# Loading the weight through GpSimd's queue instead of SyncE's, behind the first load of x

## The chip, the cores and the metric

The kernel runs on one core of a Trainium2 chip. The metric is the time of one execution on the device in microseconds, lower is better. Profiles come from one execution under the hardware profiler.

## What is computed

```python
batch, m, k, n = 16, 512, 1024, 768
def reference(x, weight, scale, add_value):
    return (scale * np.matmul(x, weight) + add_value).astype(np.float32)
```

All arrays are float32: x has 8192 rows of 1024 (33.6 MB), the weight is 1024 x 768 (3.1 MB), add_value and the output have 8192 rows of 768 (25.2 MB each). `scale` is 0.1.

## The kernel before

The 8192 rows are 64 tiles of 128 rows. x is laid out so that a partition holds 16 successive rows of a group of 2048; a load of 8 tiles (4,096 KB) therefore brings 32 KB to each partition in one run. The weight stays on the chip as eight slices of 128 x 768 in bf16 (`w_bf`). The buffers are `xs` (16 tiles of x), `ao` (32 tiles of add_value, over which the result is written in place, and whose last eight tiles first hold the float32 weight), `va` (two buffers of x in bf16, four tiles each, called a move), `xt` (four tiles of transposed x) and `mm` (four accumulators in PSUM).

Each engine has its own program, and they meet at semaphores only:

- SyncE (`sync_engine`) issues nearly all transfers, in the order of the list `STREAM`: `("w", 0, 4)` is half of the weight (slices 0 to 3), `("x", 8, 8)` eight tiles of x from tile 8 on, `"a"` is add_value, `"o"` is a store. The first load of x (tiles 0 to 7) is issued ahead of that list, at line 239. The weight is issued at line 111, x at 118, add_value at 130, stores at 143; waits ahead of them are in `need`, line 102. All of these go through one hardware queue, q1. A load of add_value waits until the one before it has landed, a load of x until the casts have freed its place.
- ScalarE and GpSimd (`mover`, cast at line 163) copy x to bf16 in eight instructions per move each, in an order that makes the later transpose work on blocks of 32 x 32. Each takes half of the partitions' blocks, and each waits for the load (`x_sem`) and for a free `va` (`turned`).
- VectorE (`vector_engine`) first casts the weight in two halves (`cast_w`, line 171), each behind the landing of its half (`w_sem`). Then it transposes the moves from `va` to `xt`, half a move per instruction (`turn`, line 178); the first half of a move waits for both movers. Between transposes it takes finished accumulators, two tiles at a time, and makes `scale * mm + ao` (`finish`, line 187).
- TensorE (`product`, line 210) waits for all eight slices of the cast weight, and then for each pair of tiles for the transposes and for free accumulators.
- GpSimd besides issues three stores of tiles 8 and 15 (`store_pair`, line 95) after its first 64 casts; they use the software queue q0. They are its only transfers.

The end of the list orders the last transfers: `("a", 56, 8), ("o", 32, 16), ("o", 48, 12), ("o", 60, 4)`. The store of tiles 48 to 59 (4,608 KB) waits for the results of tile 59, the last store (1,536 KB) for those of tile 63.

Of the kernel before, what the change touches and what calls it, by code (L numbers as in the profile page):

```python
# [16 lines left out]
VA_BUFS = 2  # L17
MOVE = 4
AHEAD = 4
HALF_BLOCK, PAST, SYNC_AT = 64, 4, 4  # L20

STREAM = [
# [13 lines left out]
def kernel(  # L36
# [8 lines left out]
    nc = tc.nc  # L45
# [15 lines left out]
    w_v = weight.rearrange("(c p r) n -> p c (r n)", p=P, r=2)  # L61

    def rows(view, s, n):
        assert s // R == (s + n - 1) // R
        return view[:, s // R, s % R:s % R + n, :]
# [5 lines left out]
    ao = const.tile([P, A_SLOTS, N], fp32, name="ao")  # L71
# [6 lines left out]
    w_sem = [tc.alloc_semaphore(f"w{i}") for i in range(2)]  # L78
    x_sem = [tc.alloc_semaphore(f"x{i}") for i in range(X_SLOTS // MOVE)]
# [8 lines left out]
    W_AT = A_SLOTS - KJ  # L88

    def slot(t):  # L90
        return t % A_SLOTS

    def store_pair(eng, p, n):
        assert PAIR.stop <= R and PAIR.stop <= A_SLOTS
        eng.dma_start(out_v[p:p + n, 0, PAIR, :], ao[p:p + n, PAIR, :]).then_inc(aside_sem, 16)  # L95

    def sync_engine(eng):
        groups, stores, known = 0, [], {}

        def need(sem, value):  # L100
            if known.get(sem, 0) < value:
                eng.wait_ge(sem, value)  # L102
                known[sem] = value

        for at, (op, s, n) in enumerate(STREAM):
            if at == SYNC_AT:
                eng.addr_align(HALF_BLOCK, offset=PAST, max_nops=0)
            last = s + n - 1
            if op == "w":
                dst = ao[:, W_AT + s:W_AT + s + n, :].rearrange("p (c r) n -> p c (r n)", r=2)  # L110
                move, sem = eng.dma_start(dst, w_v[:, s // 2:(s + n) // 2, :]), w_sem[s // 4]
            elif op == "x":
                k = s % X_SLOTS
                if last >= X_SLOTS:
                    moved = 8 * (last + 1 - X_SLOTS) // MOVE
                    need(by_act, moved)
                    need(by_pool, moved)
                move = eng.dma_start(xs[:, k:k + n, :], rows(x_v, s, n))  # L118
                sem = x_sem[k // MOVE]
            elif op == "a":  # L120
                if groups:
                    need(a_sem, 16 * groups)
                if last == A_SLOTS - 1:
                    need(casts, KJ)
                if s <= PAIR.start + A_SLOTS <= last:
                    need(aside_sem, 16 * len(BY_POOL))
                if s >= A_SLOTS:
                    i = next(j for j, (a, b) in enumerate(stores) if a <= last - 1 - A_SLOTS < a + b)
                    need(o_sem[i % 2], 16 * (i // 2 + 1))
                move = eng.dma_start(ao[:, slot(s):slot(s) + n, :], rows(add_v, s, n))  # L130
                sem = a_sem
                groups += 1
            elif op == "a+":
                need(a_sem, 16 * groups)
                eng.sem_inc(a_sem, 16 * (n // G - 1))
                groups += n // G - 1
                continue
            else:
                i = len(stores)
                if i > 1:  # L140
                    need(o_sem[i % 2], 16 * (i // 2))
                need(made, MADE + last + 1)
                move = eng.dma_start(rows(out_v, s, n), ao[:, slot(s):slot(s) + n, :])
                sem = o_sem[i % 2] if s < ENDING else end_sem
                stores.append((s, n))
            move.then_inc(sem, 16)
            if op == "x" and n == 2 * MOVE:
                eng.sem_inc(x_sem[k // MOVE + 1], 16)

    def mover(eng, copy, parity, count, go=None, first=0, turns=T // X_SLOTS):  # L150
        if go is None:
            eng.preload_act_table(mybir.ActivationFunctionType.Copy)  # L152
        with eng.Fori(16 * (first + 1), 16 * (first + turns) + 1, 16) as i:  # L153
            for q in range(X_SLOTS // MOVE):
                eng.wait_ge(x_sem[q], i)
                eng.wait_ge(turned, i + (4 * q - 12) if q < 3 else i)  # L156
                if go is not None:
                    eng.sem_inc(go, 1)  # L158
                k = MOVE * q
                src = xs[:, k:k + MOVE, :].rearrange("p i (c b k) -> p (i c) b k", b=4, k=64)  # L160
                for a in (parity, parity + 2):
                    for b in range(4):
                        copy(va[q % VA_BUFS][32 * b:32 * b + 32, :, a, :],  # L163
                             src[32 * a:32 * a + 32, :, b, :]).then_inc(count, 1)

    def vector_engine(eng):
        ao_g = ao.rearrange("p (g t) n -> p g t n", t=G)

        def cast_w(s, n):
            eng.wait_ge(w_sem[s // 4], 16)  # L170
            eng.tensor_copy(w_bf[:, s:s + n, :], ao[:, W_AT + s:W_AT + s + n, :]).then_inc(casts, n)  # L171

        def turn(move, half, moves=None):
            if half == 0:
                eng.wait_ge(by_act, moves)
                eng.wait_ge(by_pool, moves)  # L176
            q = 2 * half * KC
            eng.transpose(  # L178
                xt[:, 2 * half:2 * half + 2, :, :].rearrange("p i c m -> p (i c m)"),
                va[move % VA_BUFS][:, q:q + 2 * KC, :, :].bitcast(fp32).rearrange("p c a k -> p (c a k)"),  # L180
            ).then_inc(turned, 2)

        def finish(pair, at, products):
            eng.wait_ge(done, products)
            a = ao_g[:, at, 2 * pair:2 * pair + 2, :]
            q = 2 * (pair % 2)
            eng.scalar_tensor_tensor(  # L187
                a, mm[:, q:q + 2, 0:N], float(scale), a,
                op0=mybir.AluOpType.mult, op1=mybir.AluOpType.add).then_inc(made, 2)

        def group(i, at, last):
            eng.wait_ge(a_sem, i)
            for p in range(4):
                finish(p, at, i + (4 * p - 12) if p < 3 else i)
                if p < 2 or not last:
                    turn(1 if p < 2 else 0, p % 2, i + 8 if p == 2 else i)

        cast_w(0, 4)
        cast_w(4, 4)
        turn(0, 0, 8)  # L200
        turn(0, 1)
        with eng.Fori(16, 2 * T, 16) as i:
            group(i, bass.ds((i // 16 + A_SLOTS // G - 1) % (A_SLOTS // G), 1), False)
        s = slot(T - G) // G
        group(2 * T, slice(s, s + 1), True)
# [12 lines left out]
    def tensor_engine(eng):  # L218
        eng.sem_inc(x_sem[1], 16)
        eng.sem_inc(turned, TURNED)  # L220
        eng.sem_inc(made, MADE)
        eng.wait_ge(casts, KJ)
        with eng.Fori(TURNED + 2, TURNED + 2 + T, XT_TILES) as i:
            for q in range(XT_TILES):
                if q % 2 == 0:
                    eng.wait_ge(turned, i + q if q else i)
                    eng.wait_ge(made, i + q if q else i)
                for j in range(KJ):
                    x2 = xt[:, q, j // 2, :].bitcast(bf16).rearrange("p (m r) -> p r m", r=2)
                    m = product(eng, mm[:, q, :], x2[:, j % 2, :], w_bf[:, j, :], j)  # L230
                if q % 2:
                    m.then_inc(done, 4)
# [4 lines left out]
    s, n = FIRST  # L237
# [4 lines left out]
    with tc.tile_critical(no_gpsimd_drain=True):  # L242
        sync_engine(nc.sync)
        mover(nc.scalar, nc.scalar.copy, 0, by_act)
        mover(nc.gpsimd, nc.gpsimd.tensor_copy, 1, by_pool, pool_go, 0, TURN_AT)
        nc.gpsimd.wait_ge(made, MADE + PAIR.stop)
        for p, n in BY_POOL:
            store_pair(nc.gpsimd, p, n)
        nc.gpsimd.addr_align(HALF_BLOCK, offset=PAST, max_nops=0)
        mover(nc.gpsimd, nc.gpsimd.tensor_copy, 1, by_pool, pool_go, TURN_AT, T // X_SLOTS - TURN_AT)  # L250
        vector_engine(nc.vector)
        tensor_engine(nc.tensor)
# [40 lines left out]
```

## Time and profile before

| | |
|---|---|
| median of 3 runs | 207.01 us (206.86 to 207.15) |
| profiled execution | 206.85 us, of which the span is 205.5 us |
| DMA | 87.04 MB, mean 424 GB/s |
| busy | TensorE 167.5 us, GpSimd 137.4 us, ScalarE 134.7 us, VectorE 98.0 us |
| granted TensorE clock, mean | 0.986 |

The span runs from the first to the last recorded instruction or transfer of the execution; the rest of its time lies around it. Rows of a timeline give start, duration, engine, line, operation, tiles and count, and in brackets how long the engine was idle before and what ended that. Rows of the waits give microseconds in total, the number of times, and the longest. Rows of the queues give packets, MB, and the time that their packets took as a share of 16 engines over the span or stretch asked for. Rows of transfers give KB each and the microseconds from issue to landing.

### The profile page before, as it was taken

What the parts mean: (1) busy time and instruction counts of PE and PEld (TensorE: products, weight loads), DVE (VectorE), ACT (ScalarE), POOL (GpSimd) and SP (SyncE); (2) the same over time, 40 slices, a digit from 0 to 9 for tenths busy, and PEclk for the clock granted to TensorE, in tenths of its full rate; (3) what the DMA queues carried; (4) which work ended last, traced back from release to release, by engine and by line L of the source; (5) the groups of instructions that cost most, each with busy time, mean ns of one, the idle gap of its engine ahead of it and who ended that gap; (6) DMA issues with size and microseconds to landing.
All of it is one profiled execution on the core that took longest, in us unless ns stands there. A gap on an engine that the chain in (4) does not pass through costs nothing.

```text
span 205.5 us, 2223 instructions
## 1 busy us (share of the span) xinstructions
PE 167.5 (82%) x1008; PEld 50.4 (25%) x512; DVE 98.0 (48%) x66; ACT 134.7 (66%) x129; POOL 137.4 (67%) x135
## 2 busy tenths in 40 slices
PE   0000099999999999999999999999999997999900
PEld 0000022233322333223332233332333322333200
DVE  0004525537555555465555555555552853455330
ACT  2049980699999906999999059999991099920000
POOL 0049994699999916999999549999992099930000
PEclk9999999999999999999999999999999999999995
DMA  8989999999999899999999999999999999998997
GB/s 287 427 372 438 440 485 408 392 437 459 446 459 459 357 459 408 408 426 413 455 404 450 431 416 464 434 411 421 440 431 415 437 448 421 493 459 364 423 440 304
DMA packets 4065, 87.04 MB, mean 424 GB/s; under 512 B 480, under 2 KB 480, under 8 KB 1120
## 3 DMA queue, kind: packets, MB, share of 16 engines
q1 hardware_dynamic: 3856, 86.25, 98.1%
q0 software_dynamic: 208, 0.79, 0.9%
q14 instruction: 1, 0.01, 0.0%
HBM read 61.87 MB, written 25.17 MB: 424 GB/s over the span
## 4 chain that ended last, share of the span: by engine, by line
DMA 38%; PE 36%; POOL 10%; ACT 5%; issue 4%; DVE 3%; SPq 1%; POOLq 0%; DVEq 0%; ACTq 0%
PE mm L210 36%; DMA out_dram<-ao 22%; DMA xs<-in_x_dram 15%; POOL va L163 9%; ACT va L163 5%; DVE xt L178 2%; DVE ao L187 1%; POOL out_dram L95 1%; SPq L130 0%; SPq L118 0%; DVEq L176 0%; SPq L102 0%; POOLq L156 0%; POOLq L158 0%; POOLq L153 0%
## 5 line engine op out<-in xcount | busy, mean ns | idle before, releaser
L210 PE MATMUL mm<-w_bf,xt 128*128 128x256 bf16 (+1 forms) x1008 | 167.5, 327 | 28.0 <-DVE xt L178 27.1
L163 POOL CAST va<-xs 32x1024 bf16<-32x1024 f32 x128 | 135.2, 1056 | 44.2 <-DMA xs<-in_x_dram 36.8
L163 ACT CAST va<-xs 32x1024 bf16<-32x1024 f32 x128 | 133.4, 1042 | 45.2 <-DMA xs<-in_x_dram 42.2
L187 DVE SCALAR_TENSOR_TENSOR ao<-mm,ao 128x1536 f32 (+1 forms) x32 | 56.2, 1756 | 72.9 <-PE mm L210 68.9
L208 PEld LDWEIGHTS <-xt 128*128 128x128 bf16 x512 | 50.4, 98 | 144.6 <-issue 116.6
L178 DVE STREAM_TRANSPOSE xt<-va 128x1024 f32<-128x1024 f32 x32 | 39.4, 1234 | 8.4 <-POOL va L163 6.3
L171 DVE CAST w_bf<-ao 128x3072 bf16<-128x3072 f32 x2 | 4.5, 2240 | 18.1 <-DMA ao<-in_weight_dram 18.1
L152 ACT ACT_TABLE_LOAD x1 | 1.3, 1283 | 1.3 <-SPq L242 1.3
L95 POOL DMA_DIRECT2D out_dram<-ao x3 | 2.0, 672 | 0.0
L274 POOL MEMSET const-float32-0.0<- 128x1 f32 x1 | 0.1, 98 | 0.2 <-issue 0.2
L274 POOL MEMSET const-bfloat16-1.0<- 128x1 bf16 x1 | 0.1, 101 | 0.0
L274 POOL MEMSET const-float32-1.0<- 128x1 f32 x1 | 0.1, 98 | 0.0
L274 POOL MEMSET const-uint8-127<- 128x1 uint8 x1 | 0.1, 98 | 0.0
## 6 DMA issues: line engine op xcount, KB each, us to landing
xs<-in_x_dram SPq DMA_DIRECT2D x7, 4096.0 KB, 20.9
ao<-in_add_value_dram SPq DMA_DIRECT2D x6, 3072.0 KB, 15.7
out_dram<-ao SPq DMA_DIRECT2D x3, 3072.0 KB, 27.4
ao<-in_add_value_dram SPq DMA_DIRECT2D x1, 6144.0 KB, 24.2
out_dram<-ao SPq DMA_DIRECT2D x1, 6144.0 KB, 31.2
out_dram<-ao SPq DMA_DIRECT2D x1, 4608.0 KB, 14.9
xs<-in_x_dram SPq DMA_DIRECT2D x2, 2048.0 KB, 21.0
ao<-in_weight_dram SPq DMA_DIRECT2D x2, 1536.0 KB, 16.8
```

The costliest lines, as they stand in the source:

```text
L95: eng.dma_start(out_v[p:p + n, 0, PAIR, :], ao[p:p + n, PAIR, :]).then_inc(aside_sem, 16)
L152: eng.preload_act_table(mybir.ActivationFunctionType.Copy)
L163: copy(va[q % VA_BUFS][32 * b:32 * b + 32, :, a, :], src[32 * a:32 * a + 32, :, b, :]).then_inc(count, 1)
L171: eng.tensor_copy(w_bf[:, s:s + n, :], ao[:, W_AT + s:W_AT + s + n, :]).then_inc(casts, n)
L178: eng.transpose(xt[:, 2 * half:2 * half + 2, :, :].rearrange("p i c m -> p (i c m)"), va[move % VA_BUFS][:, q:q + 2 * KC, :, :].bitcast(fp ...
L187: eng.scalar_tensor_tensor(a, mm[:, q:q + 2, 0:N], float(scale), a, op0=mybir.AluOpType.mult, op1=mybir.AluOpType.add).then_inc(made, 2)
L208: eng.ldweights(x_j, tile_position=(0, 0))
L210: m = eng.add_instruction(mybir.InstMatmult(start_tensor_calc=(j == 0), stop_tensor_calc=(j == KJ - 1), tile_size=(P, P), tile_position=(0 ...
L274: nc = _bacc.Bacc("TRN2", target_bir_lowering=False, num_devices=1)
```

## The change

The two weight loads leave SyncE's list, and a new function `load_weight` issues them from GpSimd, with `single_packet=True`. GpSimd's program now begins with a wait for the first load of x, then the two loads, then its casts. The loads keep their destinations and their semaphores `w_sem`, so `cast_w` is unchanged. `SYNC_AT`, the place in the list at which SyncE's instructions are aligned, goes from 4 to 2, as the list is two entries shorter.

```diff
-HALF_BLOCK, PAST, SYNC_AT = 64, 4, 4
+HALF_BLOCK, PAST, SYNC_AT = 64, 4, 2
 STREAM = [
-    ("w", 0, 4), ("w", 4, 4), ("a", 0, 8),
+    ("a", 0, 8),
     ("x", 8, 8), ("a", 8, 8), ("x", 16, 8), ("a", 16, 16), ("x", 24, 8),
...
+    def load_weight(eng):
+        for s in (0, 4):
+            dst = ao[:, W_AT + s:W_AT + s + 4, :].rearrange("p (c r) n -> p c (r n)", r=2)
+            eng.dma_start(dst, w_v[:, s // 2:s // 2 + 2, :], single_packet=True).then_inc(w_sem[s // 4], 16)
...
-            if op == "w":
-                dst = ao[:, W_AT + s:W_AT + s + n, :].rearrange("p (c r) n -> p c (r n)", r=2)
-                move, sem = eng.dma_start(dst, w_v[:, s // 2:(s + n) // 2, :]), w_sem[s // 4]
-            elif op == "x":
+            if op == "x":
...
         mover(nc.scalar, nc.scalar.copy, 0, by_act)
+        nc.gpsimd.wait_ge(x_sem[0], 16)
+        load_weight(nc.gpsimd)
         mover(nc.gpsimd, nc.gpsimd.tensor_copy, 1, by_pool, pool_go, 0, TURN_AT)
```

## The prediction

> **What bounds the kernel now.** I read the page first: its engine row, the DMA row of the 40 slices, and the queues.
>
> ```profile
> span 205.5 us, 2223 instructions
> PE 167.5 (82%) x1008; PEld 50.4 (25%) x512; DVE 98.0 (48%) x66; ACT 134.7 (66%) x129; POOL 137.4 (67%) x135
> DMA  8989999999999899999999999999999999998997
> ...
> q1 hardware_dynamic: 3856, 86.25, 98.1%
> q0 software_dynamic: 208, 0.79, 0.9%
> ```
>
> The DMA engines are busy from one end to the other: 98.1% + 0.9% = 99.0% of the span, so only 2.0 us are idle. TensorE is nearly as full once it has begun, as the waits show (the first two rows over the whole span, the third for 60 to 206 us alone):
>
> ```profile
> PE mm L210 <- DVE xt L178: 27.1, 2, 26.0
> DVE w_bf L171 <- DMA ao<-in_weight_dram: 18.1, 2, 16.7
> PE mm L210 <- DVE xt L178: 1.1, 1, 1.1
> ```
>
> TensorE waits 26.0 us for its first operand and after that only once, for 1.1 us late in the run. So there are two chains of almost equal length: the transfers, which must move a fixed number of bytes, and TensorE, which runs without a break from its start. The change touches the start of the second. The timeline of the first 30 us says what sets it:
>
> ```profile
> 0.74 0.38 SPq L239 DMA_DIRECT2D xs<-in_x_dram  x1
> 1.39 0.90 SPq L111 DMA_DIRECT2D ao<-in_weight_dram  x2
> 2.34 0.56 SPq L130 DMA_DIRECT2D ao<-in_add_value_dram  x1
> 2.94 0.48 SPq L118 DMA_DIRECT2D xs<-in_x_dram  x1
> 12.89 17.04 ACT L163 CAST va<-xs 32x1024 bf16<-32x1024 f32 x16 [10.26 <-DMA xs<-in_x_dram]
> 13.04 20.27 POOL L163 CAST va<-xs 32x1024 bf16<-32x1024 f32 x16 [12.60 <-DMA xs<-in_x_dram]
> 16.65 2.31 DVE L171 CAST w_bf<-ao 128x3072 bf16<-128x3072 f32 x1 [16.65 <-DMA ao<-in_weight_dram]
> 20.40 2.17 DVE L171 CAST w_bf<-ao 128x3072 bf16<-128x3072 f32 x1 [1.44 <-DMA ao<-in_weight_dram]
> 24.69 2.37 DVE L178 STREAM_TRANSPOSE xt<-va 128x1024 f32<-128x1024 f32 x2 [2.12 <-ACT va L163]
> 26.00 24.19 PE L210 MATMUL mm<-w_bf,xt 128*128 128x512 bf16 x136 [26.00 <-DVE xt L178]
> 27.64 0.33 SPq L130 DMA_DIRECT2D ao<-in_add_value_dram  x1
> ```
>
> The four loads land in the order of the queue: x at 12.8, the weight's halves at 16.65 and 20.40 (3.75 us each), add_value's first group at 27.64 (7.25 us for 8 packets of 24 KB per engine, 0.91 us a packet). DVE casts the weight, then waits until 24.6 for the first eight casts of GpSimd, and transposes; TensorE starts 1.31 us after that transpose begins. The wait is put down to ACT, but ACT's eight were over by 12.89 + 8 x 1.065 = 21.4. GpSimd's were not:
>
> ```profile
> L163 POOL CAST va<-xs x16: 1026/1035/2452, 13.0 to 32.3; 32x1024 bf16<-32x1024 f32 x16
> ...
> 23.52 1.04 POOL L163 CAST va<-xs 32x1024 bf16<-32x1024 f32 x1
> 78.84 17.45 POOL L163 CAST va<-xs 32x1024 bf16<-32x1024 f32 x16 [6.30 <-DMA xs<-in_x_dram]
> 120.68 34.96 POOL L163 CAST va<-xs 32x1024 bf16<-32x1024 f32 x32 [4.95 <-DMA xs<-in_x_dram]
> ```
>
> The eighth ends at 24.56. Undisturbed, eight take 17.45 / 2 = 8.72 us; here they took 11.52, as two of them were stretched to some 2.45 us beside DVE's two casts of the weight.
>
> **The change, part by part.** SP loses the two weight issues (0.90 us), so add_value's first group and x's second load are issued 0.9 us earlier. They stand behind the first x load in the same queue, so SP's saving is worth nothing; the cover is the x load until 12.8. From then on the engines carry add_value instead of the weight.
>
> GpSimd's new wait ends with its old one, at 12.85. Behind it are queued two issues and then its casts. Its issues cost what its stores at 96 us do:
>
> ```profile
> 96.23 2.01 POOL L95 DMA_DIRECT2D out_dram<-ao  x3
> out_dram<-ao POOLq DMA_DIRECT2D x1, 588.0 KB, 15.1
> out_dram<-ao POOLq DMA_DIRECT2D x1, 36.0 KB, 7.4
> ```
>
> 2 x 0.67 = 1.34 us: its casts begin at 14.4 and the eighth ends at 25.9 if both DVE casts fall among them, 24.5 with one. Alone this would put TensorE's start at 25.9 + 1.35 = 27.25, a delay of 1.25 us.
>
> The large unknown is when a transfer issued by GpSimd moves its first byte. The first row below is the DMA for 0 to 1.9 us in 40 slices: SP issues at 0.74, and the first packets stand in the 37th slice, at 1.71, so 1.0 us later. The others are the queues in three stretches behind GpSimd's issue at 96.23 (96.2 to 101, 101.1 to 104, and 103.6 to 112 with both queues):
>
> ```profile
> DMA  0000000000000000000000000000000000009909
> ...
> q0 software_dynamic: 2, 0.00, 0.0%
> ...
> q0 software_dynamic: 44, 0.12, 10.1%
> ...
> q1 hardware_dynamic: 128, 3.04, 84.0%
> q0 software_dynamic: 123, 0.58, 16.7%
> ```
>
> In the first 4.8 us the queue moved nothing to speak of; then it ran at once. So I take 4.7 us from issue to first byte, under the same full traffic, and 1.0 us as the other end. The Trainium skill ("DMA: Bandwidth & Descriptors", section "Latency and other measured facts") gives about 1 us to the first byte on GpSimd's path; the rows above show nearly five times that, and by the skill's figure the delay would be that of GpSimd's casts alone, the first rival below.
>
> The last two rows also show how the queues share an engine: 123 records against 128, turn about, whatever their size. A weight half is 96 KB per engine; as one packet it holds an engine for the 3.75 us of the rows above, and between the halves one packet of add_value gets its 0.91 us. So: first byte at 12.9 + 4.7 = 17.6; the slowest engine ends its current packet at 18.5; first half until 22.25; a packet of add_value until 23.15; second half until 26.9. If the completion needs a turn of its own, 0.9 more. The bytes bound it too: add_value's first group and the weight are together done at 27.6, as before. I take 27.1 for the second landing, against 20.40.
>
> DVE then casts until 29.3 (2.2 us), and GpSimd's casts are by then over (24.5 to 25.9), so this landing is what ends last. Transpose from 29.35, TensorE from 30.65: **its start is 4.65 us later.** With the ends of the unknown: 1.25 us (first byte after 1.0 us, second half at 23.2, GpSimd last) to 5.5 us.
>
> How much of it reaches the end? The transfers are the same bytes in a queue that is never empty, and the waits of the middle have slack: GpSimd idles 6.30 us before 78.84 and 4.95 us before 120.68 waiting for x, which swallows the delay of its casts. At the end the rows are:
>
> ```profile
> 159.64 38.10 SPq L143 DMA_DIRECT2D out_dram<-ao  x3
> 185.17 1.76 DVE L187 SCALAR_TENSOR_TENSOR ao<-mm,ao 128x1536 f32<-128x1536 f32 x1 [1.98 <-PE mm L210]
> 186.96 0.34 SPq L143 DMA_DIRECT2D out_dram<-ao  x1
> 197.41 0.33 SPq L143 DMA_DIRECT2D out_dram<-ao  x1
> out_dram<-ao SPq DMA_DIRECT2D x1, 6144.0 KB, 31.2
> out_dram<-ao SPq DMA_DIRECT2D x1, 4608.0 KB, 14.9
> out_dram<-ao SPq DMA_DIRECT2D x1, 1536.0 KB, 8.1
> ```
>
> TensorE's one late stall, 1.1 us for the last x, is absorbed first. Then the store of 4,608 KB, issued when DVE's result of 185.17 is made, is late. It landed at 201.9, 11.0 us behind the store before it (159.64 + 31.2 = 190.8), so for most of its 14.9 us it stood in the queue. Alone it would need those 11.0 plus 1.0 us to start and up to 1.25 us to be acknowledged (the first x load: 12.05 us, of which 9.8 at 428 GB/s and 1.0 to start). Its slack is so 14.9 - 11.0 - 1.0 = 2.9 at most and 1.65 at least; I take 2.4, since the start and part of the acknowledgement are paid once. What is beyond leaves the engines idle, and the last store behind it moves with it. The sum: 4.65 - 1.1 - 2.4 = **+1.15 us**, on the profiled execution's 206.85 (span 205.5 and 1.35 around it) 208.0, on the median of 207.01, 0.16 above it, **208.2 us**.
>
> **The rivals.**
>
> *A quick start (not slower).* If GpSimd's first byte comes 1.0 us after its issue, as SP's does, TensorE starts 1.25 us late, of which 1.1 are the late stall's and the rest the store's slack: 207.0. The deciding point is a delay of 3.5 us (1.1 + 2.4), a second landing near 25.95. For it: in this kernel the only software transfers are those at 96 us, in mid-traffic with GpSimd's own casts right behind, and 4.7 us may be partly particular to them. Against: traffic and casts are the same at 13 us. The Trainium skill's 1 us, above, is this case.
>
> *The queue's packets stay small (far slower).* The change relies on one packet per engine. If the weight went in records of 6 KB that take turns with packets of 24 and 32 KB, it would move like the stores: 0.58 MB in 8.4 us, 69 GB/s. The 3.15 MB would need 45 us, TensorE would start about 40 us late, and after the 3.5 us of slack the time would be near 244. Against it stands that the transfer is asked for as a single packet; no row of before shows such a packet. The Trainium skill (same page, section "SWDGE vs HWDGE vs iDMA") calls packets of up to 4,096 bytes preferred, with a limit of 64 descriptors.
>
> *The transfers gain.* The whole stream has 2.0 us of idle, of which 1.7 lie before the first byte; 0.3 are left. The weight's halves run at 1.57 MB / 3.75 us = 419 GB/s against 434 for add_value; at that rate they would save 0.26 us together. A gain is so 0.56 us at most, 206.45, and only if the start is quick too. The skill's section "Issuing engines are not separate DMA queues" says that a further issuing engine saves issue time only; the 0.90 us of SP's are such time, and hidden.
>
> **How the numbers follow.** Late first byte, the forecast: 0.58, with its own range from 207.2 to 209.2 (delay of 3.7 to 5.5 us, slack 1.65 to 2.9), of which 0.05 falls within 0.2%. Quick start: 0.25, of which 0.21 is no change and 0.04 faster. Small packets: 0.07. Gain: 0.10. A change of 0.2%, 0.41 us, is about the least that a measurement of this kernel can tell from none (its runs spread by 0.29). Faster 0.14, same 0.26, slower 0.60. The range runs from 206.7, which leaves out the larger part of the gains, to 210.4, which takes in a second half that must let two of x's packets go first (delay 6.9); small packets stay outside.
>
> **What would show it.** Right: q0 moves nothing until about 17.5 and then 3.15 MB; DVE's casts of the weight start near 22.3 and 27.1; TensorE starts near 30.6; its late wait of 1.1 us is gone; the 4,608 KB store is issued near 190.5, and the engines idle just before it. Wrong: a second cast of the weight before 25.9 with GpSimd's casts as the last before the transpose (quick start), or casts of the weight tens of us apart (small packets); an idle stretch in the middle would mean that the slack there was misjudged.

## The result: 14% slower, and the profile after

The changed kernel takes 235.33 us (median of 6 runs) against 206.96 us before; the ratio is 1.137 (95% interval 1.135 to 1.138), 28.4 us more. The prediction of 208.2 us, at most 210.4, was wrong; nearest to the measured time is the rival in which the weight moves in small records (244).

The page after, with its engine row, the DMA row of the 40 slices and the queues:

```profile
span 234.4 us, 2239 instructions
PE 169.4 (72%) x1024; PEld 50.6 (22%) x512; DVE 96.6 (41%) x66; ACT 134.7 (57%) x129; POOL 136.1 (58%) x137
DMA  7999999995993079038999999999999999999898
q1 hardware_dynamic: 3312, 83.10, 84.0%
q0 software_dynamic: 752, 3.93, 4.0%
```

The transfers are no longer the bound: 84.0% + 4.0% = 88.0% of the span, and slices with 0, 3 and 7 tenths stand in its first half. TensorE is busy for as long as before (some records of before are missing) but in a longer span. The waits of TensorE and VectorE say where the time went:

```profile
PE mm L212 <- DVE xt L180: 57.4, 1, 57.4
DVE w_bf L173 <- DMA ao<-in_weight_dram: 52.7, 2, 37.4
```

The start of TensorE moved from 26.0 to 57.4 us, the wait for the weight from 18.1 to 52.7. The timeline of the start (VectorE, GpSimd, SyncE):

```profile
37.35 1.76 DVE L173 CAST w_bf<-ao 128x3072 bf16<-128x3072 f32 x1 [37.35 <-DMA ao<-in_weight_dram]
54.46 1.76 DVE L173 CAST w_bf<-ao 128x3072 bf16<-128x3072 f32 x1 [15.35 <-DMA ao<-in_weight_dram]
56.13 2.36 DVE L180 STREAM_TRANSPOSE xt<-va 128x1024 f32<-128x1024 f32 x2
...
13.10 1.59 POOL L100 DMA_DIRECT2D ao<-in_weight_dram  x2 [12.66 <-DMA xs<-in_x_dram]
14.74 17.44 POOL L165 CAST va<-xs 32x1024 bf16<-32x1024 f32 x16
...
20.82 0.33 SPq L132 DMA_DIRECT2D ao<-in_add_value_dram  x1
```

GpSimd issued the weight at 13.10 in 1.59 us and went on with its casts, as reckoned. But the halves landed at 37.3 and 54.4 instead of 16.6 and 20.4, while add_value's first group, which had stood behind the weight, was in by 20.8 (before, 27.6). The queues in two stretches, 17 to 18 us and 18 to 37 us:

```profile
q1 hardware_dynamic: 10, 0.25, 57.0%
q0 software_dynamic: 16, 0.10, 23.4%
...
q1 hardware_dynamic: 263, 6.73, 82.3%
q0 software_dynamic: 256, 1.47, 18.5%
```

In 13 to 17 us q0 does not appear; its first record of 6 KB stands in the next microsecond, at 17.45. Then there is a record of one queue for a record of the other, 263 to 256: 25.6 KB on average for SyncE, 6 KB for the weight. The weight is not one packet per engine. q0 has 544 records more than before (752 against 208) and q1 544 fewer (3312 against 3856), so the weight moves in as many records as it did in SyncE's queue. In the kernel before, the DMA from 12 to 21 us, when the weight moved, was:

```profile
DMA packets 592, 3.93 MB, mean 437 GB/s; under 512 B 48, under 2 KB 48, under 8 KB 560
```

These are 560 - 48 = 512 records of 6 KB, 16 on each of the 16 engines for each half; the other 32 of the 544 are tiny. Now each of the 16 waits for one of SyncE's. 16 turns took 37.35 - 17.45 = 19.9 us until the landing, 1.25 us each (0.23 for the weight's own record, the rest for add_value's 24 KB or x's 32 KB); the other 16 took 17.1 us.

From 57.43 on TensorE does not wait again; the chain that ended last has it as one piece, and the engines stand idle between 72 and 84 and 94 and 104 us:

```profile
57.43 169.39 PE mm L212 x1024
...
72.00:84.00 12.00, 12.00 (x76) 3.62 (x37) 7.43 (x6) 8.34 (x8) 8.28 (x8) 1.00 0.07 19
94.00:104.00 10.00, 10.00 (x63) 2.97 (x31) 5.42 (x5) 8.34 (x8) 8.27 (x8) 1.00 0.00 0
```

(The last two columns are the DMA's share and GB/s.) So a kernel with both chains full has become one that TensorE alone bounds, from a start that is 31.4 us late; 28.4 of them are in the time.

### The profile page after: what moved, and what is told of

The parts are those of the page before. It is cut to its first block, busy times and chain, and to the rows that moved or that the text cites. A ratio compares the mean times of both kernels' runs of the same rounds, so it can differ in the third digit from the quotient of the medians.

```text
span 234.4 us, 2239 instructions
## 1 busy us (share of the span) xinstructions
PE 169.4 (72%) x1024; PEld 50.6 (22%) x512; DVE 96.6 (41%) x66; ACT 134.7 (57%) x129; POOL 136.1 (58%) x137
## 3 DMA queue, kind: packets, MB, share of 16 engines
q1 hardware_dynamic: 3312, 83.10, 84.0%
## 4 chain that ended last, share of the span: by engine, by line
PE 72%; DMA 22%; DVE 1%; issue 1%; POOL 0%; DVEq 0%; POOLq 0%
PE mm L212 72%; DMA ao<-in_weight_dram 17%; DMA xs<-in_x_dram 5%; DVE ao L189 1%; DVE xt L180 1%; POOL ao L100 0%; DVE w_bf L173 0%; DVEq L204 0%; DVEq L186 0%; POOLq L158 0%; POOLq L155 0%; DVEq L172 0%; POOLq L160 0%
## 5 line engine op out<-in xcount | busy, mean ns | idle before, releaser
L212 PE MATMUL mm<-w_bf,xt 128*128 128x512 bf16 (+1 forms) x1024 | 169.4, 329 | 57.4 <-DVE xt L180 57.4
L165 POOL CAST va<-xs 32x1024 bf16<-32x1024 f32 x128 | 132.4, 1034 | 61.1 <-DVE xt L180 36.0
L173 DVE CAST w_bf<-ao 128x3072 bf16<-128x3072 f32 x2 | 3.5, 1760 | 52.7 <-DMA ao<-in_weight_dram 52.7
L100 POOL DMA_DIRECT2D ao<-in_weight_dram x2 | 1.6, 797 | 12.7 <-DMA xs<-in_x_dram 12.7
## 6 DMA issues: line engine op xcount, KB each, us to landing
ao<-in_add_value_dram SPq DMA_DIRECT2D x1, 6144.0 KB, 17.1
```

The lines of the kernel that those rows point to most:

```text
L100: eng.dma_start(dst, w_v[:, s // 2:s // 2 + 2, :], single_packet=True).then_inc(w_sem[s // 4], 16)
L165: copy(va[q % VA_BUFS][32 * b:32 * b + 32, :, a, :], src[32 * a:32 * a + 32, :, b, :]).then_inc(count, 1)
L212: m = eng.add_instruction(mybir.InstMatmult(start_tensor_calc=(j == 0), stop_tensor_calc=(j == KJ - 1), tile_size=(P, P), tile_position=(0 ...
```

## The experiments

All are compared with the kernel before, run beside them on the same chip.

**Does the flag bind anything?** The change without it:

```diff
-            eng.dma_start(dst, w_v[:, s // 2:s // 2 + 2, :], single_packet=True).then_inc(w_sem[s // 4], 16)
+            eng.dma_start(dst, w_v[:, s // 2:s // 2 + 2, :]).then_inc(w_sem[s // 4], 16)
```

> The change without single_packet, nothing else altered. Theory (turns by record): the profile after shows the weight as 512 records of 6 KB that alternate one by one with SyncE's records of 24 and 32 KB, so the flag binds nothing together: landings at 37.3 and 54.4 us as with it, 235 us, same. Rival (the flag helps in part, for instance by letting an engine's two or three records follow each other): without it the landings are later by several us, 240 us or more.

Measured: 234.89 us, ratio 1.135 (1.132 to 1.138), against 1.137 (1.135 to 1.138) with the flag. Casts of the weight start at 37.44 and 54.53; the queues have the same 752 and 3312 records. In this transfer the flag does nothing that the profile shows. Why it doesn't, no run here can say.

**Is it GpSimd's queue?** The same loads at the same point, from ScalarE:

```diff
+        nc.scalar.wait_ge(x_sem[0], 16)
+        load_weight(nc.scalar)
         mover(nc.scalar, nc.scalar.copy, 0, by_act)
-        nc.gpsimd.wait_ge(x_sem[0], 16)
-        load_weight(nc.gpsimd)
```

> The same two loads at the same point, issued from ScalarE's hardware queue instead of GpSimd's. Theory A (taking turns record by record is what costs, on whatever second queue): first byte 1.0 us after the issue, then 16 turns of about 1.2 us for each half: landings near 33 and 50, TensorE starts near 53, some 231 us. Theory B (the software queue is slow by itself, or only it is cut into records): the weight moves at full rate, landings near 18 and 23, TensorE starts near 27.3, 207 us. Theory C (ScalarE's transfers join SyncE's queue behind add_value and x): landings near 41 and 45, TensorE near 48, some 226 us.

Measured: 234.78 us, ratio 1.135 (1.132 to 1.137). The page lists a third queue (first row), the next two rows are the queues from 18 to 37 us, and the timelines of ScalarE and VectorE give issue and landings:

```profile
q10 hardware_dynamic: 544, 3.15, 3.2%
...
q1 hardware_dynamic: 264, 6.75, 83.3%
q10 hardware_dynamic: 259, 1.49, 18.8%
...
12.73 0.94 ACTq L100 DMA_DIRECT2D ao<-in_weight_dram  x2
...
37.43 1.76 DVE L173 CAST w_bf<-ao 128x3072 bf16<-128x3072 f32 x1 [37.43 <-DMA ao<-in_weight_dram]
54.53 1.76 DVE L173 CAST w_bf<-ao 128x3072 bf16<-128x3072 f32 x1 [15.34 <-DMA ao<-in_weight_dram]
```

A hardware queue of its own is as slow: both halves land within 0.1 us of those of the change, and the records again go one for one, 264 to 259. So the software queue as such is not what costs; a second queue beside a full one is. Of the three theories A's mechanism holds, but not its time to the first byte: q10 had moved nothing by 16.0, and 14 records by 17.0, so some 3.7 us after the issue, not 1.0.

**And with the first queue empty?** SyncE waits for both halves before it issues anything but the first load of x:

```diff
+        need(w_sem[0], 16)
+        need(w_sem[1], 16)
         for at, (op, s, n) in enumerate(STREAM):
```

> The change, but SyncE issues nothing after the first load of x until both halves of the weight have landed: GpSimd's queue is alone. Theory (turns): first byte 4.5 us after the issue as before, near 17.5, then full rate, 3.75 us a half: landings near 21.4 and 25.2, TensorE starts near 28.5; the engines stand idle from 12.5 to 17.5 and about 1 us after 25.2, and the end is 6 us late: 213 us. Rival (GpSimd builds its records slowly, and that sets the pace): landings stay near 37 and 54 and the time is above 235 us.

Measured: 213.65 us, ratio 1.033 (1.031 to 1.035). The row of q0 is that for 14.4 to 15.0 us; there is none in 13.0 to 14.4:

```profile
q0 software_dynamic: 10, 0.06, 70.0%
...
19.95 1.80 DVE L175 CAST w_bf<-ao 128x3072 bf16<-128x3072 f32 x1 [19.95 <-DMA ao<-in_weight_dram]
23.69 1.76 DVE L175 CAST w_bf<-ao 128x3072 bf16<-128x3072 f32 x1 [1.94 <-DMA ao<-in_weight_dram]
26.48 2.37 DVE L182 STREAM_TRANSPOSE xt<-va 128x1024 f32<-128x1024 f32 x2 [1.03 <-POOL va L167]
```

Alone, GpSimd's queue, issued at 13.10 as in the change, moves its first byte 1.6 us later, at 14.69, and its two halves land 3.74 us apart, the 3.75 of before. So the 4.7 us that the prediction read from the stores at 96 us were only in part GpSimd's own; the rest went with the other queue's traffic. The transpose now waits for GpSimd's casts, and TensorE starts at 27.8. What is lost here is DMA time: the engines idle until the weight's first byte, and again from the weight's end until SyncE's transfers follow it. The time agrees with the 213 written down, but not by its sum: the first byte came 2.9 us sooner than assumed there, and TensorE has four later waits, of 5.2 us in all, that the sum did not have.

**Is a turn one record, whatever its size?** The weight read in runs of 12 KB; its rows then come in another order than x's columns, so that the product is of permuted rows, and the run serves for its times alone:

```diff
+    w_long = weight.rearrange("(p r) n -> p (r n)", r=8)
...
-            dst = ao[:, W_AT + s:W_AT + s + 4, :].rearrange("p (c r) n -> p c (r n)", r=2)
-            eng.dma_start(dst, w_v[:, s // 2:s // 2 + 2, :], single_packet=True)
+            dst = ao[:, W_AT + s:W_AT + s + 4, :].rearrange("p t n -> p (t n)")
+            eng.dma_start(dst, w_long[:, s * N:(s + 4) * N], single_packet=True)
```

> The change, with the weight read in runs of 12 KB per partition and half instead of two of 6 KB (the weight's rows come in another order than x's columns, so the product is of permuted rows). Half as many records of the same bytes. Theory (one record per turn): 8 turns of 0.46 + 0.95 us, then 8 of 0.46 + 1.2: landings near 28.8 and 42, TensorE starts near 45, some 223 us. Rival (a fixed share of bytes or a fixed rate for the software queue): landings near 37 and 54, 235 us.

Measured: 222.54 us, ratio 1.076 (1.073 to 1.078). VectorE's timeline, and the queues from 18 to 30 us:

```profile
30.03 2.22 DVE L174 CAST w_bf<-ao 128x3072 bf16<-128x3072 f32 x1 [30.03 <-DMA ao<-in_weight_dram]
41.90 1.76 DVE L174 CAST w_bf<-ao 128x3072 bf16<-128x3072 f32 x1 [9.65 <-DMA ao<-in_weight_dram]
...
q1 hardware_dynamic: 140, 3.83, 74.7%
q0 software_dynamic: 130, 1.40, 27.8%
```

Again nearly one for one, 140 to 130, now with 12 KB a turn. There are half the turns, and the landings come within 1.3 us of the forecast.

**From the other side: SyncE's records made short.** A gap behind each tile in x's buffer cuts its loads into records of 4 KB. (The views of x in `mover` are written with one dimension more for it, without a change of the copies.) The same gap in the kernel before is the control:

```diff
-    xs = nc.alloc_sbuf_tensor("xs", [P, X_SLOTS, K], fp32).ap()
+    xs = nc.alloc_sbuf_tensor("xs", [P, X_SLOTS, K + 16], fp32).ap()[:, :, 0:K]
```

> The change, with a gap of 64 bytes behind each tile in the buffer of x, so that SyncE's loads of x are cut into records of 4 KB instead of 32 KB; the weight is as in the change. Theory (record for record): the first byte near 17.4 as before; three turns beside add_value's 24 KB records, then turns of 0.23 + 0.16 us beside x's: landings near 26 and 32.5, TensorE starts near 35.5; against its own control (the kernel before with the same gap) 6 to 7 us slower instead of 28: some 216. Rival (GpSimd's queue has a fixed share of bytes or time, about a fifth): landings near 37 and 54 as in the change, 28 us slower than its control.

> The control: the kernel before with the same gap behind each tile of x. Records of 6 KB move at 26.3 bytes per ns and engine, of 32 KB at 27.0, which extends to some 25.9 for 4 KB: the 33.6 MB of x take 3 us longer, all of it seen as the engines are full: 210 us; TensorE starts near 26 as before.

Measured: 215.09 us against the control's 209.41, so 5.7 us for the change instead of 28.4 (the two ratios to the kernel before are 1.040, 1.036 to 1.044, and 1.012, 1.010 to 1.014). The queues of the first from 22 to 30 us, and its two casts of the weight:

```profile
q0 software_dynamic: 335, 1.96, 58.8%
q1 hardware_dynamic: 335, 1.37, 42.8%
...
26.64 2.24 DVE L174 CAST w_bf<-ao 128x3072 bf16<-128x3072 f32 x1 [26.64 <-DMA ao<-in_weight_dram]
33.07 1.76 DVE L174 CAST w_bf<-ao 128x3072 bf16<-128x3072 f32 x1 [4.19 <-DMA ao<-in_weight_dram]
```

335 to 335: record for record, and this time the weight has the larger share, since its records are the longer ones. A fixed share for the second queue is excluded: it would have been as slow as in the change. The control shows what x's short records cost by themselves: 2.5 us.

**Is the late issue to blame?** GpSimd issues at once, without waiting for x:

```diff
-        nc.gpsimd.wait_ge(x_sem[0], 16)
         load_weight(nc.gpsimd)
```

> The change without GpSimd's wait for the first load of x. Theory (turns by record): issue near 0.7, first byte near 5, then 16 turns of 1.45 us beside x's records for the first half and 16 of about 1.2 to 1.45 for the second: landings near 27 and 47, the first x load about 2 us later than 12.8, TensorE starts near 50, some 228 us. Rival (the late issue, 12 us, is the whole of the loss): landings near 9 and 13, the end as before, 207 us.

Measured: 226.64 us, ratio 1.095 (1.091 to 1.099). GpSimd issues at 1.95, so 11.15 us sooner, and VectorE and ScalarE begin at:

```profile
26.50 2.50 DVE L173 CAST w_bf<-ao 128x3072 bf16<-128x3072 f32 x1 [26.50 <-DMA ao<-in_weight_dram]
46.05 1.76 DVE L173 CAST w_bf<-ao 128x3072 bf16<-128x3072 f32 x1 [17.05 <-DMA ao<-in_weight_dram]
...
14.17 17.04 ACT L165 CAST va<-xs 32x1024 bf16<-32x1024 f32 x16 [11.55 <-DMA xs<-in_x_dram]
```

The late issue accounts for 8.7 us of the 28.4 (235.33 - 226.64); the other 19.7 remain without it. x itself lands only 1.3 us later than before.

**The second half of the sum: what a late start costs.** The kernel before, with VectorE casting the second half of the weight two, three and five times more, to move TensorE's start and little else (the edit shown is that with three; beside two more, GpSimd's first 16 casts take 23.1 us instead of 20.3):

```diff
+    late = tc.alloc_semaphore("late")
...
             eng.wait_ge(w_sem[s // 4], 16)
+            for i in range(3 if s else 0):
+                eng.tensor_copy(w_bf[:, s:s + n, :], ao[:, W_AT + s:W_AT + s + n, :]).then_inc(late, 1)
+                eng.wait_ge(late, i + 1)
```

> The kernel before, with VectorE casting the weight's second half twice more: TensorE starts about 2.9 us later. The prediction's slack of 3.5 us (1.1 of the late stall, 2.4 of the store) would hide it all: 207.0, same. From the run with three more (5.3 us of delay gave 3.6 at the end, 1.7 hidden): 1.2 later, 208.1.

> The kernel before, with VectorE casting the weight's second half three times more, so that only the start of TensorE is later: about 4.5 us, the delay that the prediction reckoned with. The prediction's sum (1.1 us of the late stall and 2.4 us of the store's slack go first): end later by 1.0 us, 208.0. Theory from the result (31.4 us of delay gave 28.9 at the end, so 2.5 are hidden): later by 2.0, 209.0. Rival (no slack): 211.5.

> As the run with three more casts, with five: TensorE starts about 8.9 us later. The prediction's sum: end later by 5.4 us, 212.4. From the result's 2.5 us hidden: 6.4, 213.4. Rival (no slack): 215.9.

The waits of TensorE in the three give the starts:

```profile
PE mm L214 <- DVE xt L182: 28.8, 1, 28.8
...
PE mm L214 <- DVE xt L182: 31.3, 1, 31.3
...
PE mm L214 <- DVE xt L182: 36.3, 1, 36.3
```

| casts more | start later by | time | later than before | hidden |
|---|---|---|---|---|
| 2 | 2.8 us | 207.06, ratio 1.0005 (0.9995 to 1.0015) | 0.1 | 2.7 |
| 3 | 5.3 us | 209.99, 1.012 (1.008 to 1.017) | 3.1 | 2.2 |
| 5 | 10.3 us | 214.42, 1.036 (1.034 to 1.038) | 7.5 | 2.8 |
| (the change) | 31.4 us | 235.33, 1.137 (1.135 to 1.138) | 28.4 | 3.0 |

A delay of 2.8 us costs nothing, as the prediction's slack of 1.1 + 2.4 = 3.5 said. Beyond, 2.2 to 3.0 us are hidden in these rows, and 3.2 to 3.6, reckoned in the same way, in the runs without the flag, from ScalarE, with 12 KB and without the wait (TensorE starts at 57.5, 57.5, 44.9 and 49.0 us). The extra casts took 2.4 us each and made the delays larger than written down in advance (5.3 for 4.5, 10.3 for 8.9); with the true delays the prediction's sum gives 1.8 and 6.8. For three casts the 1.8 is inside the interval (1.6 to 3.5), as those runs spread from 208.46 to 210.51; for five it is 0.7 too low. TensorE's timeline before and with five casts more shows where that comes from:

```profile
26.00 147.37 PE L210 MATMUL mm<-w_bf,xt 128*128 128x512 bf16 x882 [26.00 <-DVE xt L178]
174.49 20.97 PE L210 MATMUL mm<-w_bf,xt 128*128 128x512 bf16 x126 [1.13 <-DVE xt L178]
...
36.27 168.83 PE L214 MATMUL mm<-w_bf,xt 128*128 128x512 bf16 x1024 [36.27 <-DVE xt L182]
```

The late stall of 1.1 us is gone. From TensorE's end to that of the span it was 205.5 - 195.5 = 10.0 us before; it is 212.7 - 205.1 = 7.6 with five casts more and 234.4 - 226.8 = 7.6 in the change, so 2.4 are hidden there. Both terms of the slack are as predicted. What differs is TensorE's own work from start to end: 168.3 us before without the stall, 168.8 here, 169.4 in the change, 168.0 without the wait (the last section has more on it).

With three casts more it is 209.1 - 199.7 = 9.4 us from TensorE's end to that of the span, so there the transfers still end late, and what they lose in the middle counts. The same stretch, 77 to 83 us, with three casts more, with five, and in the kernel before (last columns: DMA share, GB/s):

```profile
77.00:83.00 6.00, 6.00 (x39) 1.76 (x18) 3.59 (x3) 4.21 (x5) 3.98 (x4) 1.00 0.89 360
...
77.00:83.00 6.00, 6.00 (x39) 1.80 (x19) 3.71 (x4) 4.41 (x5) 4.58 (x5) 1.00 0.16 44
...
77.00:83.00 6.00, 5.95 (x38) 1.76 (x18) 3.65 (x3) 4.20 (x5) 3.98 (x4) 1.00 1.00 431
```

x's load of tiles 32 to 39 waits for casts, these for a free `va`, this for transposes, and these are paced by TensorE. With three casts more it is issued just as the queue runs dry, and some 0.7 us of transfer time are lost here; whether that is all that is missing was not tried. With five it is issued some 5 us after, and the idle engines cost nothing, since TensorE runs without a wait to the end.

## Why the prediction was wrong, by its steps

- *What bounds the kernel, and that the change acts through TensorE's start*: right. The runs with extra casts move that start in the kernel before, and the end follows it.
- *SP's saving is worth nothing; GpSimd's issues cost 1.34 us*: right, or nearly (1.59 us; casts from 14.7, where 14.4 was reckoned).
- *First byte at 17.6*: right (17.45), but not for the reason given: alone the queue needs 1.6 us, and under traffic even ScalarE's hardware queue needs 3.7. The prediction's sentence on the Trainium skill is to be read with this: its figure of about 1 us in "DMA: Bandwidth & Descriptors", "Latency and other measured facts", is nearer to the empty queue's 1.6 than to the 4.35 of the change, and the measured times decide here. The rival that went by it did not come, since SyncE's queue was full.
- **"As one packet it holds an engine for the 3.75 us"**: this is the step that failed. The rows beside it were read rightly: 123 records against 128, turn about. The change's own word, a single packet, was then trusted over them. A row of before already spoke against it: that of 12 to 21 us, above, which has the weight in records of 6 KB in SyncE's own queue. By record the second landing is 32 turns after 17.45: with 37.0 us for them, 54.46, where 27.1 was taken. The rival with this mechanism had a chance of 0.07. It was too dear at 244 because of its rate, 69 GB/s: in the stretch that it came from, a record of q0 carried 4.7 KB on average (0.58 MB in 123), as tiny records took turns there too (44 of the stretch's 251 are under 512 B); in the change it carried 5.7 KB (1.47 MB in 256), and 3.15 MB in 37.0 us are 85 GB/s.
- *GpSimd's idle time before 78 and 120 us swallows the delay*: only for small delays. With 10.3 us the engines idled in the middle, with 31.4 for some 20 us, just where "an idle stretch in the middle" had been named as the sign of a misjudged slack. It did not set the time of these runs, since TensorE ran without a wait from its start to its end in both.
- *1.1 + 2.4 us of slack*: right by its terms, 1.1 and 2.4 where TensorE ends last; 2.2 to 3.6 by the times. Had the weight landed at 27.1, the delay of 4.65 would have cost some 1 to 2.5 us, an estimate from the prediction's sum and the rows of two and three casts more, and inside the range. The forecast's own range of 207.2 to 209.2 is not what its ends give: delays of 3.7 to 5.5 us with slacks of 1.65 to 2.9 are 207.0 to 209.8.

The Trainium skill ("DMA: Bandwidth & Descriptors", section "Queues, rings and completion order") has each engine go round its queues packet by packet, and calls 9 to 17 descriptors a typical packet. The turns agree with the trace; the size does not, if one record is one descriptor, and the measured one decides here: a turn was one record, one run of memory of 4 to 32 KB, with q0 beside q1 (335 to 335) and with q10 beside q1 (264 to 259).

## What to carry to other kernels

Two queues that were both full shared the engines record for record, not byte for byte, in every pair tried here: a transfer of short runs beside one of long runs gets its records' share, here 6 of 30 to 38 KB, and a late start on top. Something urgent did best ahead in the same queue (207 us); longer records of its own (222.5), shorter ones of its rival (5.7 us over their control) or a rival that is held back (213.7) each won back a part. A flag that promises one packet is worth a run by itself before a sum rests on it.

## What the runs showed of the hardware that was not expected

- The time from issue to first byte went with the other queue as much as with the issuer: GpSimd 1.6 us with the queues empty, 4.35 beside SyncE's; ScalarE 3.7 beside SyncE's; SyncE 1.0 at the start of the kernel. An engine may hold some records of the full queue ahead of a newcomer: the difference of 2.7 to 2.8 us is three of add_value's records of 0.91, and in the run without the wait, beside x's records of 1.2 us, it is 2.5 us (issue at 1.95, first record at 6.05), two records. That is argued from the sizes alone, and not shown.
- VectorE's casts of the weight took 1.76 us with GpSimd idle. Beside GpSimd's casts they took from 1.76 and 1.80 (with SyncE held back) to 2.50 us (without the wait), so VectorE pays at times only. GpSimd paid each time: its 16 casts took 17.44 us without them, 18.86 beside one and 20.27 to 20.43 beside two.
- TensorE's first two tiles had their result taken 7.2 us after its start before (33.24 - 26.00) and 8.45 us after (65.88 - 57.43), with the same instructions. The change is not the cause: the other traces lie between 7.1 (56.12 - 49.03, without the wait) and 8.6 (34.98 - 26.39, the control with the gap), and the change without its flag has 7.7 (65.17 - 57.51). A kernel that TensorE bounds has this scatter in its time, which fits the 1.4 us by which the runs of the change spread, against 0.3 before. What sets it was not tried.
